# One level of Strassen's algorithm in the first layer's input product of a two-layer decoder step

## The chip, the core and the metric

The kernel runs on one core of one Trainium2 chip. The metric is the device time of one execution in microseconds (us). Engines are named as in the profile: PE is TensorE's matmul, PEld its weight load, DVE is VectorE, ACT is ScalarE, POOL is GpSimd, SP is SyncE, which issues the DMAs.

## The reference, cut to what is touched

Two groups of tokens share the weights: a prompt of 16 + 1024 tokens and 8 requests of 4 new tokens, 1072 tokens in all. The first layer is a gated short convolution; the second is latent attention over the prompt and over a paged cache. The change touches the first layer's input product, `h @ w_in`, and what is made of it:

```python
def conv_mixer(h, prev, w_in, conv_w, w_out):
    L = h.shape[1]
    b_gate, c_gate, u, z = jnp.split(h @ w_in, 4, axis=-1)      # h: L x 1024, w_in: 1024 x 4096
    v = c_gate * u
    vc = jnp.concatenate([prev.astype(v.dtype), v], axis=1)
    y = conv_w[0] * vc[:, 0:L]
    for k in range(1, CONV_WIDTH):
        y = y + conv_w[k] * vc[:, k:k + L]
    out = (b_gate * y * jax.nn.silu(z)) @ w_out
    return out, vc[:, L:]
```

Before it stands an RMS norm of the tokens, after it the second product with `w_out`, a norm, the residual, and the projection to the shared latent.

## The kernel before, in words

All numbers are float32. A product is made in three passes: each operand is split into a part that one pass carries exactly (`hi_of`, a copy by ACT, L69) and what is left (`lo_of`, a subtraction, L74), and a product is high x high + high x low + low x high. Every pass is a matmul of its own (`mm`, L64) and every matmul loads its 128x128 weights again: 7719 matmuls and 7719 weight loads.

**Front.** Nine blocks of up to 128 tokens are loaded, normed (`normed`, L191 scales the rows) and turned by PE (`flipped`, L201) into `hh` and `hl`: features on rows, 8 tiles of 128 features, 1074 token columns. The first two products are made in between, a chunk of 358 columns at a time, as tokens come.

**The conv stage** (the loop `for j in range(NK)`). There are 8 rows j of 128 output features; each has four products c, u, z, b. A product has 8 feature tiles x 3 passes x 3 chunks of 358 columns = 72 matmuls, so a row has 288, the stage 2304, of which 2016 belong to rows 1 to 7. Its weights (`conv_w`) are one DMA of 512 KB in runs of 512 bytes into `raw` (three buffers), multiplied by the norm's gain on POOL (L166), then split by ACT and DVE (`split_w`, eight buffers of each part). From the results: `cs` is a copy of c (ACT, L282), `vc` = u x cs (DVE out of PSUM, L284 to L286), `y` the three taps over `vc` (DVE, L289 to L291), `last` two small copies for the new state (POOL, L293, L294), then a tanh (ACT, L304), L305 on DVE and the product with `y` on POOL (L306, L307) make the SiLU path, and L310 writes the gated row j into `g`. `g` stays in SBUF through the stage. A tile pool named `ps3` holds two accumulators of three PSUM banks.

**After it** the second product goes over the nine blocks of tokens (`po`), with all eight tiles of `w_out`; these are loaded and split in the buffers of the conv weights, which come free while the last products run.

The order of instructions on each engine is set when the kernel is built: a list scheduler with a modelled timeline takes from the program's instructions those that are ready, so that work of the next row (loads, gains, splits) goes ahead of the current row's late steps. Each engine then works its queue strictly in that order. SP's queue holds all DMA issues named here, in order too.

Of the kernel before, what the change touches and what calls it, by code (L numbers as in the profile page):

```python
# [31 lines left out]
CH = TA // 3             # 358  # L32
NQ = SEQ + TS            # 1056 query columns
QCH = NQ // 3            # 352
# [15 lines left out]
def decoder_step(ctx: ExitStack, tc: tile.TileContext, i, o):  # L50
# [12 lines left out]
    def mm(out, a, b, start, stop):  # L63
        return pe.matmul(out, a, b, start=start, stop=stop)  # L64

    def hi_of(out, src, scale=1.0, eng=None):
        """the part of src that one pass carries exactly"""
        if eng is None or eng is act:
            return act.activation(out, src, AF.Copy, scale=scale)  # L69
        return eng.tensor_copy(out, src)  # L70

    def lo_of(out, src, hi, eng=None):
        """what is left of src"""
        (eng or dve).tensor_tensor(out, src, f(hi), ALU.subtract)  # L74

    def product(out, ah, al, bh, bl, start, stop):
        """out += a b, of operands in two parts"""
# [4 lines left out]
    # ---------------------------------------------------------------- constants  # L82
# [36 lines left out]
    # ---------------------------------------------------------------- layer A  # L119
    pp = ctx.enter_context(ExitStack())  # L120
    ps3 = pp.enter_context(psum("ps3", bufs=2))
# [3 lines left out]
    g = main.tile([P, NK, TA], F32, tag="g", name="g")  # L125
# [7 lines left out]
    with ExitStack() as l1:  # L133
        l0 = l1.enter_context(ExitStack())
        hp = l0.enter_context(sbuf("hp", side="right"))
        hh = hp.tile([P, NK, TA], F32R, name="hh")
        hl = hp.tile([P, NK, TA], F32R, name="hl")
# [3 lines left out]
        st_t = g[:, NK - 1, :P].rearrange("p (k c) -> p k c", c=16)  # L141
        pool.memset(f(hh[:, :, T:TA]), 0.0)
        pool.memset(f(hl[:, :, T:TA]), 0.0)
# [8 lines left out]
        def split_w(raw, eng=None, steps=1):  # L152
            wh = wp.tile([P, D], F32R, tag="wh", bufs=8, name="wh")
            wl = wp.tile([P, D], F32R, tag="wl", bufs=8, name="wl")
            for n in range(steps):
                part = slice(n * D // steps, (n + 1) * D // steps)
                hi_of(wh[:, part], raw[:, part])
                lo_of(wl[:, part], raw[:, part], wh[:, part], eng)
            return wh, wl

        def conv_w(n):
            """the products' weights in turn; the gain goes into them"""
# [10 lines left out]
        def early(b):  # L173
            if b in EARLYW:
                firsts[len(firsts)] = split_w(conv_w(len(firsts)), pool if len(firsts) in EARLYP else None, 2)
# [19 lines left out]
        def flipped(b, h, spaces=(None, None)):  # L195
            lo, r = BLOCKS[b]
            for half, pt in enumerate(spaces):
# [4 lines left out]
                ks = slice(4 * half, 4 * half + 4)  # L202
                marks["hi", b] = hi_of(hh[:, ks, lo:lo + r], pt[:, :, :r]).ins
                lo_of(hl[:, ks, lo:lo + r], pt[:, :, :r], hh[:, ks, lo:lo + r])

        def conv_mm(pt, wh, wl, chunks, ks=range(NK)):
# [1268 lines left out]
```

## Time and profile before

| | |
|---|---|
| time, median of 3 runs | 1393.22 us (1390.3 to 1394.86) |
| profiled execution | span 1391.6 us; no other time of this execution is given |
| PE busy | 1325.7 us, 95% of the span |
| DVE, ACT, POOL busy | 740.6, 599.9, 523.3 us |
| conv stage, rows 1 to 7 | 83.0 to 415.4 us |

The page counts an engine as busy while one of its instructions is open. Matmuls are pipelined, so a matmul's own duration (about 330 ns for 358 columns) is longer than the distance from one start to the next; the distance is what a matmul costs in a stream. The row groups below are from the profiled execution, and all times in them count from its start.

### The profile page before, as it was taken

The page shows a single profiled execution, that of the slowest core. Times are in us where ns is not written, and L with a number is a line of the kernel's source. Part 1 is how long each engine was busy: PE and PEld are TensorE (multiplying, and loading weights), DVE is VectorE, ACT ScalarE, POOL GpSimd, SP SyncE. Part 2 cuts the span into 40 slices and gives each one's busy share as a digit, 9 for nine tenths or more (in the row PEclk, how much of TensorE's full clock was granted, in tenths as well). Part 3 has the DMA queues.
Part 4 walks back from the last instruction along what each step waited for, and adds up shares of the span by engine and source line. Part 5 has one row for each costly group of instructions (what it writes and reads, how often), then busy time and mean ns, then how long its engine had stood idle before and what let it go on. Part 6 is the DMA issues. An engine that isn't in the chain of part 4 may idle for free.

```text
span 1391.6 us, 21275 instructions
## 1 busy us (share of the span) xinstructions
PE 1325.7 (95%) x7719; PEld 1199.3 (86%) x7719; DVE 740.6 (53%) x1509; ACT 599.9 (43%) x1191; POOL 523.3 (38%) x698
## 2 busy tenths in 40 slices
PE   7899999999999999999999999999999979899988
PEld 7899999999998888999999987878888756677776
DVE  6713221322223445317723467676787668687765
ACT  5311111111113333322232276676776678788832
POOL 5522212220011124255520365464654654455421
PEclk8999999999999999999999999999999998999999
DMA  7411111111111233134550112112212176454344
GB/s 220 122 46 46 46 47 46 41 48 35 46 46 61 91 113 93 51 107 181 196 165 16 39 24 62 43 44 47 52 35 47 27 214 173 140 154 141 107 164 175
DMA packets 97795, 123.53 MB, mean 89 GB/s; under 512 B 19976, under 2 KB 71868, under 8 KB 97692
## 3 DMA queue, kind: packets, MB, share of 16 engines
q1 hardware_dynamic: 92444, 103.31, 24.9%
q0 software_dynamic: 5248, 18.88, 4.5%
q8 instruction: 61, 1.00, 0.3%
q14 instruction: 42, 0.34, 0.1%
HBM read 89.59 MB, written 24.93 MB: 82 GB/s over the span
## 4 chain that ended last, share of the span: by engine, by line
PE 41%; DMA 8%; DVE 4%; issue 2%; ACT 2%; SPq 2%; POOL 2%; DVEq 0%; POOLq 0%; ACTq 0%
PE pa L64 10%; PE ps L64 8%; PE pm L64 6%; PE pz L64 5%; DMA qh<-qd32h 3%; PE pr L64 3%; PE pf L64 3%; PE po L64 2%; PE pc L1156 1%; PE pt L64 1%; DMA cn<-in_cache_ckv_dram,crow 1%; DMA qd32h<-qxh 1%; DMA rr<-rl 1%; PE pp L1196 1%; SPq L1140 1%
## 5 line engine op out<-in xcount | busy, mean ns | idle before, releaser
L69 ACT ACTIVATE wh<-raw 128x1024 fp32r<-128x1024 f32 (+1 forms) x66 | 57.3, 876 | 328.1 <-PE pa L64 312.0
L64 PE MATMUL pa<-hh,wh 128*128 128x358 f32 x768 | 174.8, 329 | 1.2 <-ACT cs L282 1.2
L64 PE MATMUL pa<-hl,wh 128*128 128x358 f32 x768 | 174.2, 328 | 0.0
L64 PE MATMUL pa<-hh,wl 128*128 128x358 f32 x768 | 174.0, 327 | 0.0
L74 DVE TENSOR_TENSOR wl<-raw,wh 128x1024 fp32r<-128x1024 f32 (+1 forms) x64 | 70.2, 1101 | 179.0 <-ACT wh L69 178.9
L64 PEld LDWEIGHTS pa<-hh,wh 128*128 128x128 f32 x768 | 134.3, 190 | 1.3 <-ACT cs L282 1.3
L64 PEld LDWEIGHTS pa<-hl,wh 128*128 128x128 f32 x768 | 134.4, 190 | 0.5
L64 PEld LDWEIGHTS pa<-hh,wl 128*128 128x128 f32 x768 | 133.7, 189 | 0.0
L166 POOL TENSOR_TENSOR raw<-raw,gains 128x1024 f32<-128x1024 f32 x32 | 62.3, 1953 | 129.6 <-DMA raw<-in_w_in_conv_dram 128.6
L937 ACT ACTIVATE p<-ps 128x512 f32<-128x512 f32 (+1 forms) x192 | 93.1, 492 | 38.7 <-PE ps L64 32.7
L69 ACT ACTIVATE ph<-p 128x512 fp32r<-128x512 f32 (+1 forms) x192 | 97.3, 527 | 20.5 <-POOL p L942 19.0
L64 PE MATMUL pz<-ph,v 128*128 128x512 f32 (+3 forms) x384 | 103.0, 355 | 0.4 <-ACT ph L69 0.2
L74 POOL TENSOR_TENSOR pl<-p,ph 128x512 fp32r<-128x512 f32 (+2 forms) x75 | 82.6, 1109 | 33.2 <-ACT ph L69 26.2
L74 DVE TENSOR_TENSOR pl<-p,ph 128x512 fp32r<-128x512 f32 (+3 forms) x117 | 79.8, 689 | 27.4 <-ACT ph L69 26.2
L793 DVE TENSOR_REDUCE mx<-pm 128x1 f32<-128x16 f32 (+6 forms) x210 | 83.2, 423 | 17.3 <-PE pm L64 17.0
L74 POOL TENSOR_TENSOR nl<-cn,nh 128x256 fp32r<-128x256 f32 x64 | 63.6, 1010 | 73.5 <-ACT nh L69 63.3
L942 POOL TENSOR_SCALAR_AFFINE_SELECT p<-p 128x127 f32<-128x127 f32 (+1 forms) x128 | 46.7, 368 | 77.9 <-ACT p L937 58.4
L64 PE MATMUL pm<-kh,qh 128*128 128x144 f32 (+6 forms) x210 | 60.1, 337 | 11.4 <-DMA qh<-qd32h 10.8
L64 PE MATMUL ps<-qh,kh 97*128 97x512 f32 (+3 forms) x192 | 68.2, 355 | 3.0 <-DMA qh<-mr 2.4
L64 PEld LDWEIGHTS pz<-ph,v 128*128 128x128 f32 x384 | 64.9, 189 | 7.1 <-ACT ph L69 1.2
L64 PE MATMUL pz<-pl,v 128*128 128x512 f32 (+1 forms) x192 | 67.9, 355 | 2.5 <-DVE pl L74 2.1
L64 PE MATMUL ps<-qh,kl 97*128 97x512 f32 (+3 forms) x192 | 67.0, 349 | 0.0
(344 smaller groups left out, 3157.2 us busy)
## 6 DMA issues: line engine op xcount, KB each, us to landing
raw<-in_w_in_conv_dram SPq DMA_DIRECT2D x32, 512.0 KB
raw<-in_w_in_mla_dram SPq DMA_DIRECT2D x12, 512.0 KB
raw<-in_w_out_conv_dram SPq DMA_DIRECT2D x8, 512.0 KB
x1d<-xa SPq DMA_DIRECT2D x8, 512.0 KB
qd64h<-qxh SPq DMA_DIRECT2D x8, 512.0 KB
qd64l<-qxl SPq DMA_DIRECT2D x8, 512.0 KB
qh<-qd64h SPq DMA_DIRECT2D x16, 256.0 KB
ql<-qd64l SPq DMA_DIRECT2D x16, 256.0 KB
```

The lines of the kernel that those rows point to most:

```text
L64: return pe.matmul(out, a, b, start=start, stop=stop)
L69: return act.activation(out, src, AF.Copy, scale=scale)
L74: (eng or dve).tensor_tensor(out, src, f(hi), ALU.subtract)
L166: pool.tensor_tensor(rv, rv, gains.unsqueeze(2).to_broadcast((P, NK, P)), ALU.mult)
L793: dve.tensor_reduce(mx[:, b, c:c + 1], pm[:, :off], AX.X, ALU.max)
L937: act.activation(pt[:r, :n], ps[:r, :n], AF.Exp, scale=SCALE)
L942: marks[h] = marks.get(h, []) + [pool.affine_select(pt[:r, :dn], pt[:r, :dn], [[1, dn]], ALU.is_ge, 0.0, base=META + c0 - t * P, channel_m ...
L1140: sp.dma_start(f(kp[m * DR:(m + 1) * DR]).rearrange("d r k -> d (r k)"), f(src[rr]).rearrange("d r k a -> d (r k a)"))
L1156: state["turned"] = pe.transpose(pc[:, r], cn[:, r, c * P:(c + 1) * P], ident)
L1196: pe.transpose(pp[:, n], st[:DN, g, n * P:(n + 1) * P], ident[:DN, :DN])
```

## The change

The product of rows 1 to 7 is made by the Winograd form of Strassen's algorithm. The 1024 features (the contraction) are halved, the 1072 tokens are halved (`HT` = 536 columns, two chunks of `CW` = 268), and two of the four kinds make a pair: c with u, then z with b. So a pair is a 2x2 problem whose blocks are 512 features by 128 outputs and 512 features by 536 tokens, and is made of seven products of 4 feature tiles x 3 passes x 2 chunks = 24 matmuls of 268 columns, instead of eight such blocks. Row 0 is made directly (8 tiles x 3 passes x 4 chunks x 4 kinds = 384 matmuls of 268 columns) while the token sums are formed.

- `token_sums` makes T1 to T4, four sums of token blocks, per feature tile (its temporaries `tt` share six buffers): four subtractions on POOL, six additions and subtractions on DVE, four splits (ACT and DVE), all 536 columns wide. T4 overwrites the block `12` after row 0.
- `weight_sums` makes four sums of weight blocks on POOL (512 columns) per pair and seven splits instead of two whole ones.
- Results are combined on DVE out of three PSUM accumulators a, b, c of two banks each (u2, u3, c22, c21, c12 and ACT's copies k1, c11); some products accumulate onto an accumulator that was read before.
- A row's gated result leaves for a DRAM tile `gd` (`leave`, one DMA on SP for each of rows 0 to 6) and all seven are read back into `g` by blocks of tokens, after the last row, because `T1` and `T2` lie in `g`'s place until the last pair.
- `w_out`'s split weights get a pool of their own (`wo`), in the place of the conv weights' pool and beyond, opened after that one is closed.
- The product u x c of rows 1 to 7 moves from DVE to POOL.

Comments are dropped throughout. The core of the diff:

```diff
+        def split_half(src, eng=None):
+            wh = wr.tile([P, 512], F32R, tag="wh", bufs=7, name="wh")
+            wl = wr.tile([P, 512], F32R, tag="wl", bufs=7, name="wl")
+            hi_of(wh, src)
+            lo_of(wl, src, wh, eng)
+            return wh, wl
...
+        def part(pt, ws, hs, chunks=(0, 1), start=True, stop=True, **kw):
+            for k in range(NH2):
+                for n, (a, bb) in enumerate(((0, 0), (0, 1), (1, 0))):
                     for c in chunks:
+                        marks["pe"] = mm(pt[:, c, :CW], ws[a][:, k * P:(k + 1) * P], hs[bb][:, k, c * CW:(c + 1) * CW],
+                                         start and k == 0 and n == 0, stop and k == NH2 - 1 and n == 2, **kw).ins
...
+        sums = main.tile([P, 4, NH2, HT], F32R, tag="g", name="sums")
+        H["t1"], H["t2"] = (sums[:, 0], sums[:, 1]), (sums[:, 2], sums[:, 3])
+
+        def token_sums(k):
+            q = {n: [f(t[:, k]) for t in H[n]] for n in ("11", "12", "21", "22")}
+            def less(x, y):
+                a, b = tt("ta"), tt("tb")
+                pool.tensor_tensor(a, q[x][0], q[y][0], ALU.subtract)
+                pool.tensor_tensor(b, q[x][1], q[y][1], ALU.subtract)
+                dve.tensor_tensor(a, a, b, ALU.add)
+                return a
+            def put(dst, t):
+                hi_of(dst[0][:, k], t)
+                lo_of(dst[1][:, k], t, dst[0][:, k])
+            t1 = less("12", "11")
+            put(H["t1"], t1)
+            t3 = less("22", "12")
+            put(H["t3"], t3)
+            t2 = tt("t2")
+            dve.tensor_tensor(t2, t3, q["11"][0], ALU.add)
+            dve.tensor_tensor(t2, t2, q["11"][1], ALU.add)
+            put(H["t2"], t2)
+            t4 = tt("t4")
+            dve.tensor_tensor(t4, q["21"][0], t2, ALU.subtract)
+            dve.tensor_tensor(t4, t4, q["21"][1], ALU.add)
+            return t4
...
+        def weight_sums(j, pair):
+            w1, w2 = (conv_w(4 * j + 2 * pair + n) for n in range(2))
+            a11, a12, a21, a22 = w1[:, :512], w1[:, 512:], w2[:, :512], w2[:, 512:]
+            s1, s2, s3, s4 = (wr.tile([P, 512], F32, tag="sm", bufs=4, name=f"s{n}") for n in range(1, 5))
+            pool.tensor_tensor(s1, a21, a22, ALU.add)
+            pool.tensor_tensor(s2, s1, a11, ALU.subtract)
+            pool.tensor_tensor(s3, a11, a21, ALU.subtract)
+            pool.tensor_tensor(s4, a12, s2, ALU.subtract)
+            return [split_half(x) for x in (a11, s2, a12, s3, s1, a22, s4)]
+
+        for j in range(1, NK):
+            row = Row(j)
+            for pair in range(2):
+                p1, p6, p2, p7, p5, p4, p3 = weight_sums(j, pair)
...
+                part(a, p1, H["11"])
+                act.activation(v2(k1), av, AF.Copy)
+                part(b, p6, H["t2"])
+                dve.tensor_tensor(v2(u2), bv, v2(k1), ALU.add)
+                part(a, p2, H["21"], **more)
...
+                part(b, p7, H["t3"], **more)
+                dve.tensor_tensor(v2(u3), bv, v2(k1), ALU.add)
+                part(c, p5, H["t1"])
+                dve.tensor_tensor(v2(c22), cv, v2(u3), ALU.add)
+                part(b, p4, H["t4"], **more)
+                dve.tensor_tensor(v2(c21), bv, v2(k1), ALU.add)
+                part(c, p3, H["22"], **more)
+                dve.tensor_tensor(v2(c12), cv, v2(u2), ALU.add)
+                if pair == 0:
+                    row.product(0, c21, c11)
+                    row.product(1, c22, c12)
+                    row.convolve()
+                else:
...
+                    row.gate(0, c21, out)
+                    row.silu(1, c12)
+                    row.gate(1, c22, out)
+            if j < NK - 1:
+                row.leave()
+        l2.close()
+        l0.close()
+        wr = l1.enter_context(sbuf("wo"))
+        for b, (lo, r) in enumerate(BLOCKS):
+            sp.dma_start(g[:, :NK - 1, lo:lo + r], gd.rearrange("(k p) t -> p k t", p=P)[:, :NK - 1, lo:lo + r])
...
-        wo = [split_w(load_w(i["w_out_conv"][0, k * P:(k + 1) * P])) for k in range(NK)]
```

## Rows read from the trace of the kernel before

**Rows 1.** The page: engines' busy time, and slices of the span in tenths.
```profile
PE 1325.7 (95%) x7719; PEld 1199.3 (86%) x7719; DVE 740.6 (53%) x1509; ACT 599.9 (43%) x1191; POOL 523.3 (38%) x698
PE   7899999999999999999999999999999979899988
DVE  6713221322223445317723467676787668687765
POOL 5522212220011124255520365464654654455421
```
**Rows 2.** Windows by stage: length, busy us of each engine, granted clock, DMA.
```profile
0.00:43.70 43.70, 32.72 (x188) 30.91 (x189) 29.27 (x32) 24.88 (x45) 20.95 (x35) 0.80 0.59 177
43.70:83.00 39.30, 36.42 (x225) 35.75 (x224) 21.45 (x17) 9.70 (x11) 24.09 (x16) 1.00 0.43 120
83.00:415.40 332.40, 332.40 (x2023) 331.87 (x2022) 84.88 (x85) 45.71 (x51) 66.87 (x58) 1.00 0.16 45
```
**Rows 3.** Timeline of PE and DVE in the conv stage: start us, duration us, instruction.
```profile
101.06 0.66 PE L64 MATMUL pa<-hl,wh 128*128 128x358 f32 x3
...
110.93 0.65 PE L64 MATMUL pa<-hh,wh 128*128 128x358 f32 x3
...
106.77 0.90 DVE L284 TENSOR_TENSOR vc<-pa,cs 128x716 f32<-128x716 f32 x1 [10.05 <-PE pa L64]
...
391.93 0.90 DVE L284 TENSOR_TENSOR vc<-pa,cs 128x716 f32<-128x716 f32 x1 [10.11 <-PE pa L64]
```
**Rows 4.** Timeline of PE where matmuls are 288, 256 and 144 columns wide.
```profile
523.28 0.43 PE L64 MATMUL pk<-dk,x1h 128*128 128x288 f32 x2
...
529.63 0.43 PE L64 MATMUL pk<-dk,x1h 128*128 128x288 f32 x2
...
872.58 0.40 PE L64 MATMUL pm<-up,cth 128*128 128x256 f32 x2
...
877.53 0.40 PE L64 MATMUL pm<-up,cth 128*128 128x256 f32 x2
...
1035.87 0.28 PE L64 MATMUL ps<-ql,kh 128*128 128x144 f32 x1
1035.98 0.28 PE L64 MATMUL ps<-qh,kl 128*128 128x144 f32 x1
```
**Rows 5.** Groups by line and form: busy us, mean ns, idle before (POOL, DVE, ACT).
```profile
L166 POOL TENSOR_TENSOR raw<-raw,gains 128x1024 f32<-128x1024 f32 x18 | 34.2, 1899 | 113.9 <-DMA raw<-in_w_in_conv_dram 113.9
L306 POOL TENSOR_TENSOR s<-s,y 128x1040 f32<-128x1040 f32 x7 | 17.0, 2428 | 54.2 <-DVE s L305 54.2
L307 POOL TENSOR_TENSOR s<-s,y 128x32 f32<-128x32 f32 x7 | 1.8, 254 | 0.0
L291 DVE SCALAR_TENSOR_TENSOR y<-vc,cols,y 128x1088 f32<-128x1088 f32 x7 | 9.5, 1352 | 0.2
L289 DVE TENSOR_SCALAR y<-vc,cols 128x1088 f32<-128x1088 f32 x7 | 5.5, 781 | 0.0
L74 DVE TENSOR_TENSOR wl<-raw,wh 128x512 fp32r<-128x512 f32 x2 | 1.3, 678 | 0.0
L69 ACT ACTIVATE wh<-raw 128x1024 fp32r<-128x1024 f32 x37 | 39.1, 1059 | 267.2 <-PE pa L64 253.0 <-POOL raw L166 14.2
L69 ACT ACTIVATE wh<-raw 128x512 fp32r<-128x512 f32 x4 | 2.3, 626 | 0.0
```
**Rows 6.** One tile's instructions: ns least/median/most; a 512-wide subtraction on POOL.
```profile
L74 POOL TENSOR_TENSOR wl<-uqr,wh x12: 1278/1292/2242, 597.6 to 668.3; 128x512 fp32r<-128x512 f32 x12
```
**Rows 7.** Timeline of DVE and POOL together in the front.
```profile
20.86 2.98 POOL L74 TENSOR_TENSOR wl<-raw,wh 128x512 fp32r<-128x512 f32 x2
22.60 1.27 DVE L74 TENSOR_TENSOR hl<-pt,hh 128x512 fp32r<-128x512 f32 x2
24.78 0.76 DVE L191 TENSOR_SCALAR g<-g,qa 128x1024 f32<-128x1024 f32 x1 [0.90 <-POOL qa L105]
...
30.22 5.60 POOL L166 TENSOR_TENSOR raw<-raw,gains 128x1024 f32<-128x1024 f32 x3
30.28 6.09 DVE L191 TENSOR_SCALAR g<-g,qa 48x1024 f32<-48x1024 f32 x1 [0.86 <-POOL qa L105]
...
43.11 0.62 DVE L74 TENSOR_TENSOR hl<-pt,hh 128x192 fp32r<-128x192 f32 x2
...
58.23 1.22 DVE L74 TENSOR_TENSOR wl<-raw,wh 128x1024 fp32r<-128x1024 f32 x1
58.26 2.95 POOL L166 TENSOR_TENSOR raw<-raw,gains 128x1024 f32<-128x1024 f32 x1 [1.01 <-ACT wh L69]
```
**Rows 8.** Timeline of PE after it had waited 4.60 us.
```profile
37.03 1.97 PE L201 MATMUL pt<-ident,g 128*128 128x128 f32 x8 [4.60 <-DVE hl L74]
39.39 0.50 PE L64 MATMUL pa<-hh,wl 128*128 128x358 f32 x1
39.69 0.50 PE L64 MATMUL pa<-hh,wh 128*128 128x358 f32 x1
```
**Rows 9.** Timeline of SP and POOL around one weight load, and of SP before the second product.
```profile
204.38 0.37 SPq L149 DMA_DIRECT2D raw<-in_w_in_conv_dram  x1
208.45 1.90 POOL L166 TENSOR_TENSOR raw<-raw,gains 128x1024 f32<-128x1024 f32 x1 [3.34 <-DMA raw<-in_w_in_conv_dram]
...
358.14 24.04 SPq L149 DMA_DIRECT2D raw<-in_w_out_conv_dram  x3
```
**Rows 10.** Timeline of PE where the second product begins.
```profile
414.97 0.67 PE L64 MATMUL pa<-hh,wl 128*128 128x358 f32 x3
415.48 0.63 PE L64 MATMUL po<-wh,gh 128*128 128x512 f32 x2
415.94 0.62 PE L64 MATMUL po<-wl,gh 128*128 128x512 f32 x2
```

More of the change, by code (lines that the diff above doesn't have):

```diff
@@ L31 @@
 TA = 1074
-CH = TA // 3
+HT = T // 2
+CW = HT // 2
+NH2 = 4
 NQ = SEQ + TS
@@ L61, in f, with mm @@
         return ap.bitcast(F32)
-    def mm(out, a, b, start, stop):
-        return pe.matmul(out, a, b, start=start, stop=stop)
+    def mm(out, a, b, start, stop, **kw):
+        return pe.matmul(out, a, b, start=start, stop=stop, **kw)
     def hi_of(out, src, scale=1.0, eng=None):
@@ L135, in decoder_step @@
         hp = l0.enter_context(sbuf("hp", side="right"))
-        hh = hp.tile([P, NK, TA], F32R, name="hh")
-        hl = hp.tile([P, NK, TA], F32R, name="hl")
+        pa = l0.enter_context(psum("pa"))
+        H = {jl: [hp.tile([P, NH2, HT], F32R, name=f"h{jl}{n}") for n in "hl"] for jl in ("11", "21", "22", "12")}
+        H["t3"] = [hp.tile([P, NH2, HT], F32R, name=f"ht3{n}") for n in "hl"]
         wp = l1.enter_context(sbuf("wp"))
@@ L150, in load_w, with split_w @@
             return raw
[L152 to L158, printed above, removed]
+        def split_half(src, eng=None):
[3 more added lines that the diff above has]
+            lo_of(wl, src, wh, eng)
             return wh, wl
+        def split_w(raw, eng=None):
+            return [split_half(raw[:, n * 512:n * 512 + 512], eng) for n in range(2)]
         def conv_w(n):
@@ L196, in flipped @@
             lo, r = BLOCKS[b]
+            cuts = [(lo, lo + r)] if not lo < HT < lo + r else [(lo, HT), (HT, lo + r)]
             for half, pt in enumerate(spaces):
@@ L218, in decoder_step @@
         keep_warm(turned(), WARM)
-        made = [ps3.tile([P, 3, 512], F32, tag="a", name="pa") for n in range(2)]
-        steps = [(c, n, half) for c in range(3) for n in range(2) for half in range(2)]
+        made = {(n, l): space(tag) for (n, l), tag in (((0, 0), "a"), ((1, 0), "b"), ((0, 1), "c"))}
+        steps = [(c, n, half) for c in range(4) for n in range(2) for half in range(2)]
         hs = {}
@@ L249, in decoder_step @@
         with tc.issue_after(marks["rs"]):
-            for n in range(len(firsts), 2 + 3):
+            for n in (2, 3):
                 raws[n] = conv_w(n)
@@ new lines, in decoder_step @@
+        row = Row(0)
+        evac[0, 1] = tt("c2")
+        act.activation(v2(evac[0, 1]), made[0, 1][:, :, :CW], AF.Copy)
+        for l in range(2):
+            row.product(l, made[1, l][:, :, :CW], evac[0, l])
+        row.convolve()
+        for n, l, tag in ((2, 0, "b"), (2, 1, "c"), (3, 0, "a"), (3, 1, "b")):
+            pt = space(tag)
+            for half in range(2):
+                part(pt, firsts[n][half], H[f"{half + 1}{l + 1}"], start=half == 0, stop=half == 1)
+            (row.silu if n == 2 else row.gate)(l, pt[:, :, :CW])
@@ new lines, in decoder_step @@
+        row.leave()
+        H["t4"] = H["12"]
+        for k in range(NH2):
+            t4 = token_sums(k)
+            hi_of(H["t4"][0][:, k], t4)
+            lo_of(H["t4"][1][:, k], t4, H["t4"][0][:, k])
+        def weight_sums(j, pair):
[7 more added lines that the diff above has]
+            return [split_half(x) for x in (a11, s2, a12, s3, s1, a22, s4)]
@@ new lines, in decoder_step @@
+        l2.close()
[3 more added lines that the diff above has]
+            sp.dma_start(g[:, :NK - 1, lo:lo + r], gd.rearrange("(k p) t -> p k t", p=P)[:, :NK - 1, lo:lo + r])
+        wo = []
+        for k in range(NK):
+            raw = load_w(i["w_out_conv"][0, k * P:(k + 1) * P])
+            wh, wl = (wr.tile([P, D], F32R, name=f"wo{n}{k}") for n in "hl")
+            hi_of(wh, raw)
+            lo_of(wl, raw, wh)
+            wo.append((wh, wl))
```

189 lines of the change are left out of this document (118 added, 71 removed).

## The prediction, made blind

> **What bounds the kernel now.** The page comes first: PE is open for 95% of the span and its slices stand at 9 through the part that is changed, DVE's and POOL's at 1 to 3 there [rows 1]. The windows by stage say the same of rows 1 to 7: 332.4 us, PE busy in all of them, at the full granted clock 1.00 (2.4 GHz), DVE for 84.9 and POOL for 66.9 [rows 2]. So matmuls bound this stage, and a matmul that goes is worth its distance to the next one. The timeline of PE gives that distance: from 101.06 to 110.93 us there are 20 groups of three, 60 matmuls of 358 columns, 9.87 / 60 = 0.1645 us [rows 3]. A row has 288: 47.4 us; DVE's first step on the second product comes at 106.77 in row 1 and at 391.93 in row 7, so six rows take 285.2 us, 47.5 each, and row 1 began two products (23.7) before 106.77, at 83.0 [rows 3]. The last views are of DVE and POOL, since the change turns PE's work into theirs.
>
> **Matmuls.** No matmul of 268 columns stands in this trace. 16 triples of 288 columns take 529.63 - 523.28 = 6.35 us, 0.1323 each; 14 triples of 256 take 877.53 - 872.58 = 4.95, 0.1179 each [rows 4]. Per column that is 0.459 and 0.460 ns, and 0.1645 / 358 is 0.459 too: the cost goes by columns, so 268 cost 0.1232. Bounds are the straight line between 256 and 288 (0.1233) and 0.126, should a fixed share appear. A floor is near but not reached: 144 columns start 0.11 us apart, hardly less than 256 [rows 4]. A row falls from 288 to 2 x 7 x 24 = 336 matmuls, 336 x 0.1232 + 0.2 for a transpose = 41.6 us, instead of 47.5. Rows 1 to 7: 7 x 41.6 = 291.2 against 332.4, **-41.2 us**. Row 0 costs what it did (384 x 0.1232 = 47.3).
>
> [...]
>
> **What DVE and POOL get, for a row of rows 1 to 7.** POOL: four gains x 1.90 (7.6) and eight sums of 512 columns x 1.28 [rows 5, 6] (10.2); the product u x c, moved from DVE, and the one with y, 2.7 each (2.43 + 0.25 [rows 5]); copies about 0.6. Sum 23.8 us. DVE: 14 subtractions for the splits x 0.64 (0.68 alone [rows 5], 0.635 in a chain, by the two in 1.27 us [rows 7]) = 9.0; the taps, 0.78 + 2 x 1.35 = 3.5 [rows 5]; two gates and one SiLU step that now read SBUF, 3 x 0.66 = 2.0; and out of PSUM ten adds and a SiLU step, 11 x 0.66 = 7.3. Sum 21.8. ACT: 14 splits x 0.63 and six evacuations, about 12.6. Each is far below 41.6 and would hide behind PE.
>
> But DVE and POOL don't run side by side. While POOL made three gains in a row (30.22 to 35.82), a DVE scaling whose like takes 0.76 us took 6.09: it waited for all three. At 58.23 it is the other way: a DVE subtraction with both inputs in SBUF runs 1.22 us, and POOL's gain beside it takes 2.95 instead of 1.90. A DVE instruction that reads PSUM and SBUF isn't touched: two of them take 1.27 us at 22.60 during POOL's work [rows 7]. So POOL's 23.8 and DVE's 9.0 + 3.5 + 2.0 = 14.5 exclude each other: 38.3 of 41.6 us. The Trainium skill (SBUF — State Buffer, section Who interferes with whom) says this of DVE instructions with two SBUF inputs against POOL's reads, the later one blocked until the other ends; this trace agrees (6.09 us), and it is the rule that speaks against this change.
>
> DVE works in order. Its adds out of PSUM have one product, 24 x 0.1232 = 2.96 us, until PE needs the accumulator back (u2, u3, c22); c21 and c12 have longer. POOL's bursts (a gain and three sums, 1.9 + 3 x 1.28 = 5.7) can hold a split in front of such an add. The buffers break them: s1 of the pair after next needs the buffer that the split of p5 frees, so that POOL must let that split through. I take 1.3 us of stall a row in six rows: **+7.8**. The bounds are 0, and DVE and POOL one after the other throughout: 23.8 + 21.8 = 45.6, that is 4.0 a row.
>
> **Token sums.** They can't start before the last tokens are turned and split, at 43.11 + 0.62 = 43.7 us [rows 7]. Per feature tile POOL has 4 subtractions of 536 columns, 1.28 x 536 / 512 = 1.34, or 1.30 in a chain; DVE has six adds and four splits x 0.63, all from SBUF. Up to the last tile's T2, which row 1's second product p6 needs, POOL has 16 x 1.30 = 20.8 and DVE 37 x 0.63 = 23.3: 44.1 us that exclude each other. In the same time the same two engines have row 0's taps 3.4, its product with y 2.7, copies 0.8, a gain 1.9, row 1's four weight sums 4.9 and three splits 1.9: 15.6. 43.7 + 59.7 = 103.4 with nothing lost; with 5% lost to handshakes 106. PE is done with row 0 near 76 (before: 83.0, when the next row began) and reaches the last quarter of p6 at 81, so PE waits some 25 us. What is then made of row 1 is 1.75 products, 5.2 us, so the stage stands as if row 1 had begun at 106 - 5.2 = 100.8: **+17.8**. After its wait PE is at half clock: after 4.60 us idle, 358 columns took 0.30 us each [rows 8] (granted clock 0.80 over the front [rows 2]) for some ten matmuls: **+1.4**. Bounds: 100 to 115 us for T2.
>
> **After the last row.** Before, PE went from the stage into the second product without a gap (414.97, 415.48 [rows 10]), the split weights lying ready; their loads had been issued from 358 us on at the pace of the rows [rows 9]. After, three things are late. `g` comes back by nine DMAs, 3.84 MB in 512-byte runs, which wait for T1's last use, two products (5.9 us) before the end, and fill SP's queue and the DMA engines. One load of 0.5 MB alone took 208.45 - 204.38 = 4.07 us to its first user [rows 9], so the first block is there in time; all nine, at the 300 GB/s that a share of 0.59 with 177 GB/s stands for [rows 2], take 13 us, until some 8 us after the end. And `w_out`'s first split tile lies where p3 lies, the last product's weights: its ACT and DVE steps (1.06 + 1.2 [rows 5, 7]) start only at the end. `raw` has three buffers, so tiles 3 to 7 come through them behind `g`'s loads. By that tile 7 is split some 16 to 18 us after the end, where PE would want it at 8 x 1.37 = 11 less one step (six 512-column matmuls a tile, 0.46 a pair [rows 10]). Price 6.5 to 10; I take **+8**. Bounds 4 (splits only) and 14 (loads strictly behind one another).
>
> The seven DMAs to `gd` (0.55 MB in 41 us) and the unchanged weight loads cost nothing: the DMA engines' share is 0.16 in this stage [rows 2]; SP's loads queued behind a late one have a pair's time, 20 us.
>
> **Sum**: -41.2 + 7.8 + 17.8 + 1.4 + 8 = -6.2. On the execution profiled: 1391.6 - 6.2 = 1385.4 us. The median of the runs lies 1.6 above that span; 1387 us.
>
> **Rivals.**
> *The shared path of DVE and POOL doesn't bind.* If the sums overlap, POOL alone is at 43.7 + 20.8 + 10.3 = 75 and DVE alone at 43.7 + 23.3 + 3.4 + 1.9 + 4 = 76: PE doesn't wait, and row 1 begins 7 us earlier than before. -41.2 - 7 + 8 = -40: 1353 us. Against it stands the 6.09 [rows 7]. Half of it, row stalls of 0 and T2 at 100, gives -20: 1373.
> *Rows at the pace of DVE and POOL*, the one on the other side: splits held by POOL delay an add out of PSUM, PE waits in every pair. For it: 38.3 of 41.6 us leaves little, and DVE is strictly in order. Against it: the weights are a whole pair ahead. At 45.6 a row it costs 6 x 4 = 24 instead of 7.8: +10, 1403 us. It decides from 1.3 + 6.2 / 6 = 2.3 us of stall a row.
> *The reload is longer*: if SP's order puts all of `w_out` behind `g`, each tile waits for its own load (8 x 4.07 = 33 us less the 11 in use = 22): +8, 1401 us.
> *No difference*, terms cancelling within 4 us.
>
> **Chances and range.** As summed, somewhat faster: 0.35. The shared path binds less: 0.15. Rows at DVE's pace: 0.25. Reload, or T2 near 115: 0.10. Cancelling: 0.15. What a measurement of this kernel can tell from no change is about 0.3%, 4.2 us. The sum's own spread reaches over that line, so 0.04 of its 0.35 is taken to "same": faster 0.46, same 0.19, slower 0.35. Low end: T2 at 100 (-6), no stalls (-7.8), 4 at the end (-4): 1369, reaching a little into the first rival. High end: T2 at 115 (+9), stalls of 4 (+16), 12 at the end (+4): 1416. The likeliest case alone: 1378 to 1396.
>
> **What would show it.** Right: matmuls of 268 columns 0.123 us apart; a wait of PE of 20 to 30 us in p6 of row 1, ended by the split of T2; rows 1 to 7 of 42 to 44 us; DVE and POOL instructions of 0.7 and 1.3 us stretched to 2 and more next to one another; a wait of PE at the second product, ended by a split of `w_out`. Wrong: PE through row 0 into row 1 without a wait; rows over 45 us, with waits ended by DVE's adds; or other distances between matmuls.

## The result, and the profile after the change

Before 1393.99 us (median of 4 runs), after 1406.63 (median of 4 runs): ratio 1.0091, 95% interval 1.0063 to 1.0119. The change is slower by 0.9%, where the forecast was 1387. The medians are 12.6 us apart, the two profiled executions, 1391.6 and 1406.2 us, 14.6; the sums below go by the latter.

First the page of the kernel after, engines and slices, against [rows 1]:

```profile
PE 1305.4 (93%) x8151; PEld 1175.6 (84%) x8151; DVE 897.4 (64%) x1689; ACT 646.2 (46%) x1304; POOL 657.9 (47%) x797
PE   7957999999989999999999999999999978999998
DVE  5796767566655445316833377677777677777865
POOL 5784667666511124244420265464664643555421
PEclk9977999999999999999999999999999989999999
```

PE has more matmuls (8151 for 7719), is open for 20 us less, and the span is longer: time went into gaps and into a lower clock. The third and fourth slices (70 to 141 us) show it: PE at 5 and 7, clock at 7, DVE at 9 and 6, POOL at 8 and 4. The windows by stage, against [rows 2]:

```profile
43.70:83.00 39.30, 34.08 (x275) 33.32 (x274) 31.60 (x30) 9.37 (x17) 31.60 (x21) 0.99 0.15 41
83.00:411.80 328.80, 304.91 (x2359) 300.51 (x2359) 220.98 (x240) 84.71 (x145) 198.92 (x153) 0.95 0.21 60
411.80:522.90 111.10, 105.39 (x475) 84.70 (x474) 56.75 (x60) 43.98 (x66) 17.24 (x41) 0.97 0.41 130
522.90:1406.20 883.30, 827.23 (x4816) 725.50 (x4814) 560.49 (x1327) 483.64 (x1030) 389.86 (x550) 0.97 0.34 100
```

Rows 1 to 7 end at 411.8 us instead of 415.4, and PE is idle for 24 us of that stage, where it was busy throughout. The second product's end (the first latent product, `pk`) comes at 522.9 instead of 517.1: +5.8. From there to the end the code is unchanged, yet it takes 883.3 us instead of 874.5 (1391.6 - 517.1): +8.8. Nothing in the prediction stands for that second part.

The matmuls themselves went as worked out. PE's timeline in row 2, in groups of two:

```profile
159.01 0.41 PE L66 MATMUL a<-h21h,wh 128*128 128x268 f32 x2
...
164.67 0.41 PE L66 MATMUL b<-ht3h,wl 128*128 128x268 f32 x2
```

Between the two stand 46 matmuls of 268 columns: 5.66 / 46 = 0.123 us, as scaled from [rows 3, 4]. The Trainium skill (TensorE: Matmul & The Clock Gate, section Back-to-back issue gap) has N/2.4 + 2.5 ns for the gap of an isolated matmul, an estimated 114 ns for 268 columns; in this stream, with a weight load for every matmul, the measured 123 ns counts.

**The start of row 1.** PE's timeline from 60 to 123 us, the longer waits and the first matmul of p7; in brackets the idle time before and what ended it:

```profile
86.98 0.82 PE L66 MATMUL a<-h11h,wh 128*128 128x268 f32 x2 [8.31 <-DVE s L390]
95.67 0.85 PE L66 MATMUL b<-sums,wh 128*128 128x268 f32 x4 [2.38 <-DVE s L390]
103.20 0.81 PE L66 MATMUL c<-sums,wh 128*128 128x268 f32 x2 [2.86 <-DVE sums L76]
108.67 0.81 PE L66 MATMUL b<-sums,wh 128*128 128x268 f32 x2 [4.21 <-ACT sums L71]
110.36 0.82 PE L66 MATMUL b<-sums,wh 128*128 128x268 f32 x2 [0.88 <-DVE sums L76]
116.74 0.81 PE L66 MATMUL b<-sums,wh 128*128 128x268 f32 x2 [2.37 <-ACT sums L71]
...
122.70 0.52 PE L66 MATMUL b<-ht3h,wh 128*128 128x268 f32 x2 [0.43 <-DVE u L437]
```

The first two waits are for row 0's gate (L390), a DVE instruction that reads PSUM and is quick in itself, but stands in DVE's queue behind token sums. The others are for T2 and T1, feature tile by feature tile: PE's queue has p5, which reads T1 into `c`, ahead of p2. When p7 begins at 122.70, four products are made: p1, p5, p6 and p2, 96 matmuls, 11.8 us. So the row stands as if it had begun at 110.9, where before it began at 83.0: 27.9 us late, the half clock behind the waits included. The forecast had 19.2. (Two of the expectations below have 28.7, counted from p2 as if only two products had been made by then.)

What DVE and POOL did meanwhile, their rows from the timeline:

```profile
87.93 1.81 DVE L320 TENSOR_TENSOR t<-h21h,t 128x536 f32<-128x536 f32 x1
89.13 1.80 POOL L302 TENSOR_TENSOR ta<-h12h,h11h 128x536 f32<-128x536 f32 x1
89.67 1.84 DVE L76 TENSOR_TENSOR sums<-t,sums 128x536 fp32r<-128x536 f32 x1
90.90 1.80 POOL L303 TENSOR_TENSOR tb<-h12l,h11l 128x536 f32<-128x536 f32 x1
91.43 1.82 DVE L76 TENSOR_TENSOR wl<-raw,wh 128x512 fp32r<-128x512 f32 x1
```

Each instruction is open for 1.8 us, its own 0.6 (DVE) or 1.25 (POOL) and the other's: they take strict turns. The Trainium skill's rule (SBUF — State Buffer, section Who interferes with whom), that a DVE instruction with two SBUF inputs contends with a POOL instruction that reads SBUF, holds here, as in the gain of 2.95 us in [rows 7]. The 6.09 us of [rows 7], which the prediction puts beside this rule, is a scaling with one tensor and a column of factors as inputs.

**The rows.** All of PE's waits from row 1's second product to the last row, in us, times, longest:

```profile
PE pt L362 <- POOL last L360: 4.9, 5, 1.8
PE b L66 <- DVE u L437: 1.6, 6, 0.4
```

The first is the transpose of the 18 last tokens for the new state: its place in PE's queue comes before POOL has copied them. With what is lost around these waits, the stretch from 122.7 to 411.8 us, 289.1, is 9.7 us over what was left of 7 x 41.6 (279.4); the forecast had 7.8.

**After the last row.** PE's last matmul of the rows begins at 411.77, its first of the second product at 417.22. ACT's timeline between:

```profile
411.74 1.06 ACT L71 ACTIVATE gh<-g 128x1024 fp32r<-128x1024 f32 x1 [10.62 <-DMA g<-gd]
412.84 0.65 ACT L376 ACTIVATE s<-u 128x536 f32<-128x536 f32 x1
413.39 2.93 ACT L71 ACTIVATE woh<-raw 128x1024 fp32r<-128x1024 f32 x3
416.23 1.13 ACT L71 ACTIVATE gh<-g 128x896 fp32r<-128x896 f32 x2
```

The cast that PE waits for (128x896, the first block of tokens) is the last of the four: ahead of it in ACT's queue stand another block's cast, which waited for its DMA, row 7's tanh and three casts of `w_out`. With a second wait, of 0.5 us, for `w_out`'s low part and matmuls at half clock until 424, the second product ends 9.4 us later than its own length would have it; the forecast had 8.

So by the forecast's own list: matmuls -41.2, start +27.9 (forecast 19.2), rows +9.7 (7.8), after the last row +9.4 (8), and +8.8 (no term) behind it: +14.6.

### The profile page after: what moved, and what is told of

The parts are those of the page before. It is cut to its first block, busy times and chain, and to the rows that moved or that the text cites. A ratio compares the mean times of both kernels' runs of the same rounds, so it can differ in the third digit from the quotient of the medians.

```text
span 1406.2 us, 22702 instructions
## 1 busy us (share of the span) xinstructions
PE 1305.4 (93%) x8151; PEld 1175.6 (84%) x8151; DVE 897.4 (64%) x1689; ACT 646.2 (46%) x1304; POOL 657.9 (47%) x797
## 4 chain that ended last, share of the span: by engine, by line
PE 40%; DMA 9%; DVE 4%; issue 2%; ACT 2%; POOL 1%; SPq 1%; DVEq 0%; POOLq 0%; ACTq 0%
PE pa L66 10%; PE ps L66 7%; PE pm L66 6%; PE pz L66 6%; PE pr L66 3%; PE pf L66 3%; DMA qh<-qd32h 3%; DMA cn<-in_cache_ckv_dram,crow 2%; PE po L66 2%; PE pc L1327 1%; PE pt L66 1%; DMA qd32h<-qxh 1%; DMA kp<-kh 1%; DVE big L789 1%; DMA rr<-rl 1%
## 5 line engine op out<-in xcount | busy, mean ns | idle before, releaser
L71 ACT ACTIVATE wh<-raw 128x512 fp32r<-128x512 f32 x74 | 46.0, 630 | 145.9 <-PE pa L66 49.8
L76 DVE TENSOR_TENSOR wl<-raw,wh 128x512 fp32r<-128x512 f32 x72 | 68.6, 957 | 65.1 <-ACT wh L71 64.8
L71 ACT ACTIVATE wh<-s 128x512 fp32r<-128x512 f32 x56 | 35.4, 632 | 107.7 <-PE b L66 56.5
L66 PE MATMUL ps<-ql,kh 97*128 97x512 f32 (+3 forms) x192 | 66.7, 348 | 0.0
L66 PE MATMUL pa<-x1h,wh 128*128 128x352 f32 x288 | 64.8, 332 | 0.0
L66 PE MATMUL pa<-x1h,wl 128*128 128x352 f32 x288 | 64.7, 332 | 0.0
L66 PE MATMUL pa<-x1l,wh 128*128 128x352 f32 x288 | 64.4, 332 | 0.0
L105 POOL TENSOR_SCALAR ta<-ss 128x1 f32<-128x1 f32 (+1 forms) x36 | 8.8, 245 | 111.5 <-ACT xa L544 51.0
```

The costliest lines, as they stand in the source:

```text
L66: return pe.matmul(out, a, b, start=start, stop=stop, **kw)
L105: pool.tensor_scalar(t[:r], ss[:r], 1.0 / n, EPS, ALU.mult, ALU.add)
```

## The experiments

Each was timed against the kernel before on the same chip. Stage times are read from the profiled executions: "rows end" is the second product's first matmul, "rest" the time from the first latent product to the end.

| kernel | ratio to before, 95% interval | span | rows end | rest |
|---|---|---|---|---|
| before | | 1391.6 | 415.5 | 874.5 |
| after | 1.0091 (1.0063 to 1.0119) | 1406.2 | 417.2 | 883.3 |
| row1_direct | 1.0040 (1.0020 to 1.0059) | 1398.4 | 403.3 | 889.4 |
| pair2_later | 1.0103 (1.0068 to 1.0137) | 1408.9 | 417.8 | 885.6 |
| cast_first | 1.0155 (1.0122 to 1.0188) | 1411.7 | 416.3 | 888.6 |
| last_later | 1.0083 (1.0055 to 1.0111) | 1402.6 | 414.8 | 882.7 |
| before_warm | 1.0011 (0.9993 to 1.0029) | 1392.4 | 418.0 | 872.8 |
| no_tsums | 0.9882 (0.9850 to 0.9914) | 1376.5 | 384.0 | 887.6 |
| no_wsums | 1.0057 (1.0036 to 1.0079) | 1396.3 | 405.6 | 885.6 |
| best | 0.9936 (0.9916 to 0.9956) | 1383.6 | 393.8 | 884.7 |
| before_swap | 1.0078 (1.0052 to 1.0104) | 1406.7 | 413.9 | 891.2 |
| after_right | 1.0083 (1.0058 to 1.0108) | 1400.7 | 415.3 | 879.8 |
| best_right | 0.9864 (0.9838 to 0.9890) | 1370.4 | 391.4 | 874.1 |
| pair2_none | 1.0107 (1.0061 to 1.0153) | 1410.2 | 413.3 | 890.7 |

### The start

**Token sums left out** (no_tsums).

```diff
+        H["t3"] = H["t4"] = H["12"]
         for k in range(NH2):
-            t4 = token_sums(k)
...
+            for n in range(2):
+                hi_of(H["t2"][n][:, k], f(H["11"][n][:, k]))
...
```

> The token sums are left out: T1 and T2 are plain ScalarE copies of a quarter's two parts, T3 and T4 the quarter itself, so that the output isn't the product. Theory A (the token sums on VectorE and GpSimd make row 1 late): of the 28.7 us that row 1 begins late, the first waits (8.6 us until row 0's gate is through, and all those for sums) go, and the first output product begins 22 to 28 us sooner, at 389 to 395 us. Rival B (row 1's own weight sums and splits would hold it up just as long): it begins less than 10 us sooner. What follows the layer is not compared, as its order may change.

The second product began at 384.0 us, 33.2 sooner, more than either theory said, and no wait of over 0.9 us was left between row 0 and row 2. So without the token sums there is no late start: row 1's own weights alone don't hold it up.

**Row 1's second weight pair behind the token sums** (pair2_later).

```diff
+                    if (j, pair) == (1, 1):
+                        for n in ("pool", "dve", "act"):
+                            l.enter_context(tc.issue_after(marks["sum " + n]))
                     p1, p6, p2, p7, p5, p4, p3 = weight_sums(j, pair)
```

> Row 1's second weight pair (gains, four sums, seven splits) is queued behind the last token sum on GpSimd, VectorE and ScalarE. Theory A (the order: this work, some 15 us of the two engines that exclude each other, stands between the token sums and delays them): the second token sum is ready some 10 to 15 us sooner, at about 105 instead of 117.9, and the time falls by 8 to 12 us to about 1396. Rival B (the amount: the two engines have no free time in the first 118 us, and what is put back is missed by row 1's second pair): the waits move to the second pair of row 1, and the time stays within 3 us of 1406.6.

Theory A fell: the last wait for T2 came at 115.42 instead of 116.74, and the rows ended 0.6 us later. POOL's last token subtraction was through at 101.35, but POOL's gains and sums, now right behind it, took turns with the ten steps that DVE still had up to T2's last split, which ended at 116.1. A new order on the queues gained nothing here, since the two engines share the path.

**The same pair without its POOL work** (pair2_none).

```diff
+            w1, w2 = (conv_w(4 * j + 2 * pair + n, (j, pair) != (1, 1)) for n in range(2))
...
+            if (j, pair) == (1, 1):
+                return [split_half(x) for x in (a11, a22, a12, a11, a21, a22, a12)]
```

> Row 1's second weight pair goes without its two gains and four sums on GpSimd (3.8 + 5.1 = 8.9 us of work); its seven splits stay, of the raw quarters, so that the output isn't the product. Theory A (the forecast's term for the token sums was too small because it left out the second pair's preparation, which GpSimd and VectorE do ahead of the second token sum's end): the last wait for the second token sum, at 116.74 us, comes 6 to 9 us sooner, at 108 to 111, and the output product begins as much sooner, at 408 to 411. Rival B (what is missing is the late start of the token sums at 53.5 us instead of 43.7, and the chain of each tile's steps): it comes less than 3 us sooner.

PE's last wait for T2 in this kernel's timeline:

```profile
107.88 0.82 PE L66 MATMUL b<-sums,wh 128*128 128x268 f32 x2 [2.36 <-ACT sums L71]
```

107.88 for 116.74: 8.9 us sooner, the 8.9 us of POOL work left out. So it is the amount of shared work ahead of T2 that counts, and the second pair's preparation belonged into the sum. Only 3.9 us of it reached the rows' end: row 2's transpose of the last tokens now waited 4.0 us for POOL.

**Row 1 made directly too** (row1_direct). Its products are made as row 0's; `last_sum` makes T4 behind it, from T2's two parts.

```diff
+        row = Row(1)
+        for n in range(4):
+            ws = split_w(conv_w(4 + n))
+            for l in (1, 0) if n == 3 else (0, 1):
...
+                    evac[l] = tt(f"c{l + 1}")
...
+        for k in range(NH2):
+            last_sum(k)
-        for j in range(1, NK):
+        for j in range(2, NK):
```

> Row 1 is made by its eight half-size products too, so the token sums need not be ready before row 2. Theory A (most of the loss is the start: row 1 begins some 28.7 us late because its first sevenfold products wait for the token sums): the waits before row 1 go, row 1 costs 5.9 us more of matmuls, and the sums hide behind it: 1406.6 - 28.7 + 5.9 = about 1384, and no wait over 2 us in front of row 2. Rival B (VectorE and GpSimd are the pace of everything up to the last row): the wait only moves to row 2 and the rows, and the time stays at 1400 or more. What follows the layer is the same code in both; if its time is as after the change (883 us from the first latent product to the end) it belongs to the change, if it moves by several us it goes by the order that the scheduler happens to choose.

The rows ended 14.0 us sooner, not 22.8. The wait for T2 was gone, but PE waited 6.7 us for ACT's copy of c, whose `tt` buffer was still held by the token sums, and 2.7 for the last tokens of row 1. The whole came out at 1.0040, since the rest took 889.4 us.

### The rows

**The last tokens' transpose later** (last_later). `tail` holds the transpose, its copy and the two DMAs.

```diff
+                if pair == 1:
+                    with tc.issue_after(marks["pe"]):
+                        row.tail()
                 part(c, p5, H["t1"])
```

> The one transpose per row that turns the last tokens (new convolution state) stands behind the second pair's fourth product instead of behind the first pair. Theory A (the rows' stalls are TensorE's in-order wait at that transpose, 4.9 us in five rows, and the 1.6 us that follow at the next product): rows 2 to 7 run at 41.7 to 42.3 us and the time falls by 4 to 6.5 us to about 1401. Rival B (the forecast's: GpSimd and VectorE are the pace of the rows, 38.3 of 41.6 us plus their waits): the stalls come back at another product, the rows stay at 42.9 to 44.3 us, and the time stays within 2 us of 1406.6.

Half of each: the waits at the transposes were gone, the rows ended 2.4 us sooner, and a wait at p7 grew. PE's waits from 118 us to the last row:

```profile
PE b L66 <- DVE u L442: 5.0, 5, 1.4
```

p7 writes the accumulator that DVE must first read for u2, and in DVE's queue u2 stood behind the first two of the three long taps of the row's convolution.

**Weight sums left out** (no_wsums).

```diff
-            pool.tensor_tensor(s1, a21, a22, ALU.add)
...
+            s1, s2, s3, s4 = a21, a22, a11, a12
```

> The weight sums are left out: their places are taken by the quarters themselves, gains and splits stay, so that the output isn't the product. That takes 8 x 1.28 us of GpSimd from each of rows 1 to 7. Theory A (TensorE's in-order wait at the last tokens' transpose makes the rows 43 us instead of 41.6, and the start is late for work shared by GpSimd and VectorE): the start is some 5 to 10 us sooner, the rows gain under 1 us each, the output product begins at 405 to 412 us. Rival B (the forecast's rival, GpSimd and VectorE are the pace of the rows): rows 2 to 7 fall to 41.7 us each and the output product begins at 400 us or sooner.

405.6 us: 11.7 sooner, of which 4.6 at the start (last wait for T2 at 112.15) and 7.1 in the rows, whose waits fell from 6.5 to 1.4 us. That is more than theory A had for the rows and less than B: with less on POOL no wait for the last tokens was left, and those for u2 shrank to 1.4 us.

### After the last row

**The first block's cast ahead of `w_out`'s** (cast_first). `out_weights` holds the loads and splits of `w_out`.

```diff
         parts = {0: gated(0)}
+        with tc.issue_after(marks["cast"]):
+            out_weights()
```

> The split of the first block of the gate is queued ahead of the splits of the output weights and of the other blocks on ScalarE. Theory A (the 5.4 us pause before the output product is ScalarE's order: the cast of 128x896 at 416.23 stands behind three weight casts and another block's cast, with its data long there): the product begins about 4 us sooner, at some 413.3 us, and its half-clock stretch shortens by 1 to 3 us: 1399 to 1402. Rival B (the pause is the reload from HBM that the change brought): the cast waits for the transfer at its new place, and the time stays within 1 us of 1406.6.

The timeline of DVE in this kernel:

```profile
417.20 1.28 DVE L76 TENSOR_TENSOR gl<-g,gh 128x896 fp32r<-128x896 f32 x2
418.41 3.49 DVE L76 TENSOR_TENSOR wol<-raw,woh 128x1024 fp32r<-128x1024 f32 x3
```

PE's pause fell from 5.45 to 3.76 us and was ended by `woh`; but PE's second wait, for `wol`, grew from 0.5 to 2.2 us behind the two `gl` on DVE. From the last matmul of the rows to `pk` it took 110.6 us instead of 111.2. So the pause's first part was ACT's order, not the transfer, but behind it stands the split of `w_out`, whose tiles come free with the last matmul. The kernel was slower in all because of the rest (888.6).

### The rest, where no code changed

The kernels with the sevenfold product took 882.7 to 890.7 us there, as long as nothing else was moved. **The kernel before, shifted** (before_warm):

```diff
-WARM2 = 18
+WARM2 = 58
```

> The kernel before, with 40 further identity transposes in front of its first products (58 for 18), nothing else; its first layer may begin up to some 9 us later. What is read is the time from the first latent product to the end, 874.5 us in the kernel before and 882.7 to 889.4 us in the five kernels with the sevenfold product, whose code is the same there. Theory A (the order of that part is chosen anew by the scheduler whenever anything ahead of it shifts, and the order of the kernel before is a lucky one): it becomes some 3 to 12 us longer here too. Rival B (the sevenfold product's own traces, such as its buffer in HBM or the places of its tiles, cost the time there): it stays at 874.5 within 1.5 us.

872.8 us: theory A fell. The scheduler did choose another order on every engine, and it cost nothing. That pointed to something that the others share. One candidate is a part of the diff that is not quoted ahead: the tile pool `ps3` of the second product is opened only after the rows, so that `pst`, the two PSUM tiles of the transposes, is opened ahead of it and lies in banks 0 and 1 instead of 6 and 7. **That part alone, in the kernel before** (before_swap), and **undone** in the kernel after (after_right) and in the fastest one so far (best_right):

```diff
-    ps3 = pp.enter_context(psum("ps3", bufs=2))
     pst = pp.enter_context(psum("pst", bufs=2))
+    ps3 = pp.enter_context(psum("ps3", bufs=2))
```
```diff
-    pst = pp.enter_context(psum("pst", bufs=2))
+    pst = pp.enter_context(psum("pst", bufs=2, side="right"))
```

> The kernel before, with one part of the change alone: the two PSUM tiles of the transposes (pst) are opened ahead of the six banks of the products, so that they lie in banks 0 and 1 instead of 6 and 7, as after the change; nothing else. Theory A (the time after the first layer grows because the attention's first score tiles, four buffers from bank 0 on, now lie where the last transposes still are, and wait for them; the pauses of 1.5 and 1.3 us ahead of the prompt's attention stand in every kernel with the change and in none without): the time from the first latent product to the end goes from 874.5 to 880 to 888 us, and the pauses at that place appear. Rival B (the cause is another part, such as the gate's buffer in HBM): 873 to 876 us, and no such pauses.

> The kernel after, with the two PSUM tiles of the transposes at the other end (banks 6 and 7, as in the kernel before); nothing else. Theory A (their place costs the 8.8 us after the first layer): from the first latent product to the end 873 to 878 us instead of 883.3, no pauses ahead of the prompt's attention, the layer itself as before at 522 to 524 us: 1396 to 1401. Rival B (another cause): 882 us or more, 1405 to 1410.

> The fastest kernel so far (row 1 directly, convolution and last transpose later in each row; 1387.5 us) with the transposes' PSUM tiles in banks 6 and 7 as well. Theory A: from the first latent product to the end 873 to 878 us instead of 884.7, the layer as there at 498 to 500 us: 1374 to 1380 us, 1.0 to 1.5% faster than the kernel before. Rival B: 883 us or more, 1386 to 1390.

before_swap is 0.8% slower than before. Its rest is 16.7 us longer, more than theory A's upper end. The prompt's attention opens four score tiles (`pm`) from bank 0 on. PE's timeline just ahead of the first, after:

```profile
797.84 0.42 PE L66 MATMUL pt<-kh,qh 96*128 96x344 f32 x1 [1.11 <-DVE mx L964]
799.17 0.27 PE L972 MATMUL pt<-ident,m 128*8 128x128 f32 x1 [0.90 <-DVE m L970]
799.80 0.80 PE L66 MATMUL pm<-up,cth 128*128 128x256 f32 x2 [0.36 <-ACT mr L977]
```

the same place in before_swap:

```profile
790.22 0.42 PE L64 MATMUL pt<-kh,qh 96*128 96x344 f32 x1 [1.11 <-DVE mx L793]
791.55 0.27 PE L801 MATMUL pt<-ident,m 128*8 128x128 f32 x1 [0.90 <-DVE m L799]
792.18 0.51 PE L64 MATMUL pm<-up,cth 128*128 128x256 f32 x2 [0.36 <-ACT mr L806]
```

and in best_right:

```profile
768.37 0.40 PE L66 MATMUL pt<-kh,qh 96*128 96x348 f32 x1 [0.28 <-DVE mx L1005]
768.61 0.40 PE L66 MATMUL pm<-up,cth 128*128 128x256 f32 x2
```

With `pst` in the way, the last maxima (`mx`) and the transposes of `m` have to be through before `pm` can begin, and PE idles three times, 2.4 us. With `pst` at the other end `pm` begins without them. That is the part that can be pointed at. By stage, from `pk` to `pm` and from `pm` to the end: before 272.1 and 602.4 us, before_swap 276.7 and 614.5, after 276.9 and 606.4, after_right 276.1 and 603.7, best 277.0 and 607.7, best_right 272.3 and 601.8. In two kernels out of three undoing or making this one swap moves the rest by 11 to 17 us, most of it behind `pm`, where many short waits for gathers and scores change; which of them follow from the swap wasn't traced one by one.

The windows from `pk` to the end, of before, after and before_swap, say in what form the time goes:

```profile
517.12:1391.60 874.48, 822.41 (x4816) 718.02 (x4814) 558.53 (x1327) 484.85 (x1031) 396.41 (x552) 0.98 0.34 100
522.94:1406.20 883.26, 827.19 (x4816) 725.50 (x4814) 560.45 (x1327) 483.64 (x1030) 389.86 (x550) 0.97 0.34 100
515.52:1406.70 891.18, 833.48 (x4816) 730.77 (x4814) 560.06 (x1327) 484.90 (x1031) 394.79 (x551) 0.96 0.33 98
```

In before_swap PE idles 5.6 us more than before, and the same 4816 matmuls are open for 11.1 us longer, at a mean granted clock of 0.96 for 0.98. In the kernel after it is 4.0 and 4.8. So at least half of what the rest loses is not in the waits themselves but in matmuls at a lower mean clock. All ten kernels with `pst` in the low banks took 882.7 us or more, the four with it at the other end 879.8 or less.

In the kernel after the swap's undoing gave only 3.5 us in the profiled executions, a rest of 879.8 between the two theories, and 1.0083 for 1.0091, no difference that the runs can tell. There the latent stage keeps another loss. The 15 us behind PE's wait for the turn of the latents (3.4 us from one start to the next), windows of after_right, then of best_right (2.9 us):

```profile
557.00:572.00 15.00, 14.68 (x83) 14.51 (x84) 8.03 (x31) 4.15 (x15) 6.10 (x9) 0.85 0.25 71
```
```profile
530.60:545.60 15.00, 14.91 (x96) 14.37 (x97) 9.11 (x32) 5.79 (x17) 6.24 (x10) 1.00 0.25 70
```

A mean granted clock of 0.85 is the lower level, 1.2 GHz, for 30% of it: 13 matmuls fewer in the same time.

### A version that beats both

**Row 1 directly, and three waits taken away** (best). The transpose of the last tokens stands behind p7, as in last_later.

```diff
-                    evac[l] = tt(f"c{l + 1}")
+                    evac[l] = row.y[:, l * HT:(l + 1) * HT]
...
-                dve.tensor_tensor(v2(u2), bv, v2(k1), ALU.add)
+                ins = dve.tensor_tensor(v2(u2), bv, v2(k1), ALU.add).ins
+                if pair == 1:
+                    with tc.issue_after(ins):
+                        row.convolve()
```

> Row 1 directly as in the earlier run, with its first product copied out into the row's own y instead of a buffer that the token sums use too (there TensorE waited 7.0 us for that copy), each row's convolution on VectorE queued behind the second pair's first sum, and the last tokens' transpose behind the second pair's fourth product. Theory A (waits by order, which each of these removes): row 1 gains 6 to 9 us, rows 2 to 7 about 0.8 us each; the output product begins at about 389 to 393 us instead of 403.3; with 982 to 990 us from there on, as the kernels so far show, 1372 to 1383 us: faster than the kernel before. Rival B (VectorE, busy 40.0 of 40 us from 60 to 100, keeps its pace and the waits move on): the output product begins at 399 us or later, and the time is 1390 or more.

The rows ended at 393.8 us, 0.8 us beyond theory A's upper end, and the kernel takes 1387.5 us, more than A said, but 0.64% less than before. With the swap undone (best_right) it is 1373.89 us, 1.36% faster. Its windows, rows 2 to 7 and the pause behind them:

```profile
125.00:384.50 259.50, 259.50 (x2106) 259.33 (x2105) 169.68 (x186) 68.47 (x118) 161.78 (x126) 1.00 0.22 65
384.50:391.40 6.90, 0.32 (x3) 0.10 (x1) 2.77 (x4) 5.29 (x7) 1.46 (x2) 0.85 1.02 268
```

PE is busy through all 259.5 us of the rows, and from row to row it takes 41.6 us, as the matmuls alone give, with DVE busy for 169.7 and POOL for 161.8. The pause behind the rows is the next thing to take away.

## Why the prediction was wrong

**Where it failed: the token sums' term, and a term that wasn't there.** The forecast's -6.2 became +14.6, 20.8 us apart: 8.7 at the start, 8.8 in the rest, 1.9 in the rows, 1.4 after them.

*Token sums, "+17.8" and "+1.4": measured 27.9.* The step that failed is "In the same time the same two engines have row 0's taps 3.4, its product with y 2.7, copies 0.8, a gain 1.9, row 1's four weight sums 4.9 and three splits 1.9: 15.6." The two exclude each other as forecast, and from 60 us on DVE was at it without a break of note (POOL had one of 4.4 us and was through with its subtractions at 109.1). But the list of what else they do before T2 is done was too short: it had one gain, four weight sums and three splits of row 1. The groups of the kernel after from 43.7 to 118 us have four gains, twice each of the four sums, and five and five splits:

```profile
L171 POOL TENSOR_TENSOR raw<-raw,gains 128x1024 f32<-128x1024 f32 x4 | 9.0, 2249 | 9.4 <-DMA raw<-in_w_in_conv_dram 9.4
L76 DVE TENSOR_TENSOR wl<-raw,wh 128x512 fp32r<-128x512 f32 x5 | 7.5, 1508 | 4.8 <-ACT wh L71 4.8
L76 DVE TENSOR_TENSOR wl<-s,wh 128x512 fp32r<-128x512 f32 x5 | 6.5, 1298 | 0.4 <-ACT wh L71 0.4
L422 POOL TENSOR_TENSOR s<-raw,s 128x512 f32<-128x512 f32 x2 | 3.4, 1710 | 0.7 <-DVE wl L76 0.7
```

At the forecast's own prices that is 3 x 1.9 + 4 x 1.28 + 7 x 0.64 = 15.3 us more: the second pair's preparation, more splits and a gain of row 2. With them the forecast's sum is 43.7 + 59.7 + 15.3 = 118.7; T2's last split ended at 117.9, where 106 was forecast:

```profile
117.17 0.71 DVE L76 TENSOR_TENSOR sums<-t,sums 128x536 fp32r<-128x536 f32 x1
```

no_tsums (33.2 us gone) and pair2_none (8.9 us sooner for 8.9 us of work left out) show it for the larger part; the other 6.4 us of the 15.3 are counted in the trace, and no run left them out. Of the 11.9 us that T2 was late some 3 came back: when p2 began, 68 matmuls of row 1 were made, p5's among them, 2.8 products where the forecast had 1.75. The stated start of the token sums (43.7) was off too; POOL's timeline has 53.45, behind a gain that waited for its load and three sums of row 1:

```profile
46.77 1.90 POOL L171 TENSOR_TENSOR raw<-raw,gains 128x1024 f32<-128x1024 f32 x1 [9.43 <-DMA raw<-in_w_in_conv_dram]
...
53.45 1.78 POOL L302 TENSOR_TENSOR ta<-h12h,h11h 128x536 f32<-128x536 f32 x1
```

Those sums were in the list, so only the 3 us until the load came are new. The forecast also overlooked that row 0's gate, in DVE's queue, would be held up: 8.3 us of PE's waiting stands there; it ends before T2 does and so adds nothing to it.

*The rest, no term: +8.8.* The forecast stopped where the changed code stops. A pool that is opened later was in the diff, and with it a new place for `pst`. before_swap shows that this alone costs the kernel before 0.8%, best_right that undoing it gives back all of it there. For the kernel after, undoing it gave 3.5 of the 8.8 us in the profiled executions, which the runs can't tell from nothing; so there the cause stays open for the most part. The half clock behind the latent stage's wait is seen in the trace, in after as in after_right; why the wait is longer there than in best_right was not tried. What remains is spread over the attention.

**What was right.** *Matmuls*, -41.2: 0.123 us each, and 41.6 us a row where nothing else holds PE (best_right). *Row stalls*, +7.8: measured 9.7, but for another reason than the one given. The rival that DVE and POOL set the rows' pace is out: the rows ran at 41.6 us with all their work in place once two orders were changed (best), and no_wsums shows the work's share, in how late the last tokens and u2 come (waits of 6.5 us against 1.4). *After the last row*, +8: measured 9.4. `w_out`'s splits were part of it, as said; that ACT would cast another block, and three tiles of `w_out`, before the one PE needs, was not foreseen, and in cast_first the first block's cast waited for the tanh ahead of it, not for the reload.

The range held the time, in part by luck: its high end stood for T2 near 115 us, which is about what came, but also for 16 us more of stalls that didn't come, and 8.8 us that no term stands for took up some of that room. The side was wrong because the two terms added up.

## What to carry to other kernels

Where two engines exclude each other, add up everything that both have to do before the due time, the next stage's preparation included, and not only what is needed: a scheduler that puts early what is ready fills the path with it. When pools are opened in another order, look at who takes their place later, however far behind the change; a stage without a changed line can lose more than the change gains (row1_direct: 8.1 us sooner at `pk`, 14.9 us longer behind it). An in-order wait of 1 us in each row was here a matter of where two small instructions stand in their queues, and both had to be moved: with one alone (last_later) the wait came back at another product.

## What the runs showed of the hardware

- DVE and POOL in alternation: instructions of 0.6 and 1.25 us alone are open for 1.8 us each (most of those from 86 to 104 us); a page that counts open instructions shows DVE at 9 tenths while much of it is waiting.
- The clock after a pause of PE doesn't go by the pause's length alone: at the same place in the latent stage, the 15 us behind a pause had a mean granted clock of 1.00 after 2.65 us (best), 2.75 (before) and 2.92 (best_right), but 0.89 after 2.52 (before_swap) and 0.81 after 3.43 (after).
